# Gated delta rule in a hybrid decoder block: the keys' matrix split from the queries', blocks of 32 instead of 16, and another projection order

## The chip, the cores and the metric

One core of one Trainium2 chip runs the whole kernel. The metric is device microseconds of one execution. The kernel before takes 711.61 us, the median of three runs from 710.02 to 714.58 us. Everything is float32 at the edges; the large products run as three passes over a high and a low part (`mm3`), and what is called f32 below on TensorE without such a split runs as two instructions for each matmul.

## The reference

One layer of a decoder block over 1024 tokens of width 1024. Half of the mixer is stick-breaking attention (8 heads of 64), half a gated delta rule (4 heads of 128, chunks of 64 in the reference):

```python
h = rmsnorm(x, norm1_w);  proj = h @ w_in                     # 1024 x 4104
sb_q, sb_k, sb_v, sb_z, g_q, g_k, g_v, g_z, g_b, g_a = split(proj)
# stick-breaking: A[t,s] = sigmoid(z_ts) * prod_{s<j<t} (1 - sigmoid(z_tj)),  o = A v
# delta rule, after a causal convolution of 4 taps, silu, and l2norm of q and k:
a_mat = where(strict, (k_beta @ k.T) * decay, 0)              # of one chunk
sol   = triangular_solve(a_mat + eye, [v_beta, k_beta*exp(g)], unit lower)
attn_intra = where(incl, (q @ k.T) * decay, 0)
for chunk: v_new = u - w @ S;  o = (q*exp(g)) @ S + attn_intra @ v_new
           S = S*exp(g_last) + (k*exp(g_last-g)).T @ v_new
x = x + concat(rmsnorm(o_sb)*silu(sb_z), rmsnorm(o_gdn)*silu(g_z)) @ w_out;  return rmsnorm(x)
```

## The kernel before

The kernel writes chunks of 128 tokens, so a delta head has 8 chunks, treated as two units of 4 (`g` = 0 and 1; unit `u = 2h+g`). All work is written as generators ("streams"): the scan over chunks (`delta_scan`, priority 0), the inversion (`delta_solve`), the substitution (`delta_blocks`), what precedes them (`delta_pre`), attention, the projections (`fill`, priority 100), and the output product (`product`, 101). A recording layer (`Model`) prices each instruction with `cost`, lets the streams go on when what they wait for has ended by these prices, and so fixes the order of every engine's instructions at build time. On the chip each engine then runs its list in order and waits on semaphores. All recorded instructions carry line L316, so rows are told apart by the names of their tiles.

Projections run in the order of `ORDER`: `v0`, `v1` are halves of attention's values with gates' columns, `k0`..`k3` attention's keys (two heads each), `G0`..`G3` a delta head (three column blocks: k, then q, then v; kinds 1, 0, 2), `z0`..`z7` the output gates. Each column block is 48 TensorE matmuls of 512 columns in two halves. Its weights are split by ScalarE (`weh`) and GpSimd (`wel`). TensorE gets its matmuls from attention and the delta rule as they become ready, and from the projections in between; attention starts when `v1` and the decays are done.

One delta head goes through these steps:

- `gdn_norms`: transposes of k and q (`kq`), squares summed by ScalarE, one reciprocal root for both (`rkq`).
- `gdn_pre`: for each chunk one matmul of k against k and q together (256 columns), from it the negated keys' matrix `nm` (in the buffer `dt`) and the queries' matrix `at`. It starts when the head's k, q and (part of) v are projected.
- `gdn_blocks`: the 32 diagonal blocks of 32x32 of a head (8 chunks, 4 blocks each) go to DRAM (`bd`) and come back with a block's matrix on the partitions that work on it (`br`). `xs` is the inverse being built by forward substitution, two columns a step: a product `tm` over what is there, then a sum of it. The kernel before inverts the two 16x16 halves of each block this way (8 steps, `tm` of 32 to 256 columns, all on VectorE), and joins the halves with two groups of 32 small matmuls: `y0p` (tile rows `pz<-wc,dt`, 16 rows) and `x0p` (`pz<-yt,xc`).
- `gdn_inv`, for each unit: joins blocks of 32 to 64 and to 128 (`xinv`) with small matmuls, starting with `pz<-wc,dt` of 32 rows; `gdn_chain`: the scan over 4 chunks.

`product` multiplies the mixed outputs by `w_out` in 8 token blocks of 128. Its first two blocks take the halves in the order (0, delta half), (1, delta half), (0, attention half), (1, attention half); the sums of block 0 stand in the two PSUM buffers `pp` that the projections use too, those of block 1 in `pz`. The weights of the attention half (`wol`) are split after the last projection, in the memory of the projections' input.

Of the kernel before, what the change touches and what calls it, by code (L numbers as in the profile page):

```python
# [17 lines left out]
P = 128  # L18
T = 1024
D = 1024  # L20
NB = T // P
# [8 lines left out]
ORDER = "v0 k0 v1 G0 k1 G1 k2 G2 G3 k3 z0 z1 z2 z3 z4 z5 z6 z7".split()  # L30
# [393 lines left out]
def block(tc, xT_d, x_d, n1_d, wE_d, wQ_d, wC_d, conv_d, alog_d, dtb_d, mixw_d, wo_d, fnw_d, out_d):  # L424
# [4 lines left out]
    with ExitStack() as top:  # L429
# [23 lines left out]
        n1 = cst.tile([P, NK], F32, name="n1")  # L453
        conv = cst.tile([P, 12, 4], F32, name="conv")
        mixw = cst.tile([P, NK], F32, name="mixw")
        alog = cst.tile([P, GH], F32, name="alog")
        dtb = cst.tile([P, GH], F32, name="dtb")
        x0 = cst.tile([P, 8, 16], F32, name="x0")
        low = cst.tile([P, 1], F32, name="low")
        rstd = cst.tile([P, NB], F32, name="rstd")  # L460
        rs8 = cst.tile([P, NB], F32, name="rs8")
        ns8 = cst.tile([P, NB], F32, name="ns8")
        rbc = cst.tile([P, T], F32, name="rbc")
        make_identity(nc, ident)
        sel = cst.tile([P, P], F32, name="sel")
        V.memset(sel, 0.0)
# [5 lines left out]
        rkq = cst.tile([P, GH, 2, NB], F32, name="rkq")  # L472
# [12 lines left out]
        xd0 = dr.tile([16, 16], F32, name="xd0")  # L485
        xds = [dr.tile([32 * 1024 + 528], F32, name=f"xd{i}") for i in range(2)]
# [53 lines left out]
        ones, triu, zero = [sm[:, i * P:(i + 1) * P] for i in range(3)]  # L540
# [68 lines left out]
        def row_scale(half, dgs):  # L609
            rp = pz()  # L610
            for g, dg in enumerate(dgs):
# [4 lines left out]
        S.dma_start(xd0, ident[0:16, 0:16])  # L616
        S.dma_start(x0.rearrange("p r i -> p (r i)"),
                    xd0.rearrange("(g r) i -> g (r i)", g=2).unsqueeze(0).to_broadcast([64, 2, 128]))
        V.tensor_reduce(low, ident.rearrange("p (q u i) -> p q u i", u=2, i=16)[:, :, 1, :], AX.XY, ALU.add)
        V.memset(zero, 0.0)  # L620
        for t in xds:
            for u in range(2):
                S.dma_start(t[16384 * u:16384 * u + 16384].rearrange("(p f) -> p f", p=P), zero)
# [7 lines left out]
        xs = gd.tile([P, 8, 32], F32, name="xs")  # L631
        edge = gd.tile([P, 3], F32, name="edge")
        for t in (*xinv, w64, xs):
            G.memset(t, 0.0)
# [31 lines left out]
        def decays(me):  # L666
# [41 lines left out]
            for h in range(GH):  # L708
                for g in range(2):
                    hc = slice(4 * g, 4 * g + 4)  # L710
                    dt = gd.tile([P, 4, P], F32, tag=("at", "nkv")[g], bufs=3, turn=True, name="dt")
# [77 lines left out]
        def projections():  # L789
# [30 lines left out]
            while nxt:  # L820
# [7 lines left out]
                for half in range(2):  # L828
# [15 lines left out]
                    if half == 0:  # L844
                        if name[0] == "G":
# [32 lines left out]


        def delta_blocks():  # L880
            for h in range(GH):
                yield lambda: h == 0 or f"i{2 * h - 1}" in flags
# [10 lines left out]
        def delta_scan():  # L893
# [7 lines left out]
            rq = rkq[:, :, 1]  # L901
# [9 lines left out]
        def gdn_norms(h):  # L911

            ss = gd.tile([P, 2, NB], F32, tag="ss", name="ss")
            kns = []
            for g in range(2):
                kq = gst[h]["kq"][g]
                kns.append(gd.tile([P, 4, P], F32, tag="kn", bufs=4, turn=True, name="kn"))
                for which in range(2):
                    tp = pz()
                    for j in range(4):  # L920
                        TE.transpose(tp[:, j * P:(j + 1) * P], kq[:, j, which, :], ident)
                    if which == 0:
                        A.activation(kns[g].rearrange("p c d -> p (c d)"), tp, AF.Copy)

                    for j in range(4):
                        js = tp[:, j * P:(j + 1) * P]
                        A.activation(js, js, AF.Square, accum_out=ss[:, which, 4 * g + j:4 * g + j + 1])
                    yield
            V.tensor_scalar(ss, ss, EPS, None, ALU.add)
            rr = rkq[:, h]  # L930
            _rsqrt(V, gd, rr.rearrange("p a c -> p (a c)"), ss.rearrange("p a c -> p (a c)"), 2 * NB, "rru")
            r2b = gd.tile([P, NB], F32, tag="r2b", bufs=2, turn=True, name="r2b")
            V.tensor_tensor(r2b, rr[:, 0, :], rr[:, 0, :], ALU.mult)
# [3 lines left out]
            nk = gd.tile([P, NB], F32, tag="nk", name="nk")  # L937
            V.tensor_tensor(nk, ss[:, 0, :], rr[:, 0, :], ALU.mult)
# [6 lines left out]

        def gdn_pre(h, g):
            st = gst[h, g]
            kq, vt = gst[h]["kq"][g], gst[h]["vt"]
            kn, nk, mr2b = st["kn"], st["nk"], st["mr2b"]
            cs = slice(4 * g, 4 * g + 4)  # L950
            dt = gd.tile([P, 4, P], F32, tag="dt", bufs=2, name="dt")
            S.dma_start(dt, dt_s[h, g])
            nkv = gd.tile([P, 4, P], F32, tag="nkv", bufs=3, turn=True, name="nkv")
            S.dma_start(nkv, cum_s[1, h, cs].partition_broadcast(P))
            nm = dt
            at = gd.tile([P, 4, P], F32, tag="at", bufs=3, turn=True, name="at")
            for i in range(2):
                gpt = pz()
                for j in range(2):
                    c = 2 * i + j  # L960
                    TE.matmul(gpt[:, j * 256:(j + 1) * 256], kq[:, c, 0, :], kq[:, c, :, :].rearrange("p a t -> p (a t)"),
                              start=True, stop=True)
                gv = gpt.rearrange("p (j a t) -> p j a t", j=2, a=2)
                V.tensor_tensor(at[:, 2 * i:2 * i + 2, :], gv[:, :, 1, :], dt[:, 2 * i:2 * i + 2, :], ALU.mult)
                for j in range(2):
                    c = 2 * i + j
                    r = V.scalar_tensor_tensor(nm[:, c, :], gpt[:, j * 256:j * 256 + P], mr2b[:, c:c + 1], dt[:, c, :], ALU.mult, ALU.mult)
                yield
            st.update(nkv=nkv, nm=nm, at=at)
            flags[f"p{2 * h + g}"] = r  # L970
# [6 lines left out]
            for j in range(4):  # L977
                A.activation(nkv[:, j, :], tp[:, j * P:(j + 1) * P], AF.Copy, scale=nk[:, j:j + 1])
            flags[f"q{2 * h + g}"] = r
            yield  # L980

        def gdn_blocks(h):
            bd = dr.tile([32, 32, 32], F32, tag="bd", bufs=2, name="bd")
            xd = xds[h % 2]
# [5 lines left out]
            br = gd.tile([P, 16, 32], F32, tag="br", name="br")  # L990
            bf = br.rearrange("p k i -> p (k i)")
            for u in range(2):
                S.dma_start(bf[64 * u:64 * u + 64, 0:496],
                            bd.rearrange("n k i -> n (k i)")[:, 528 * u:528 * u + 496].unsqueeze(1).to_broadcast([32, 2, 496]))
            V.memset(bf[:, 0:496:66], 0.0)
            V.memset(bf[:, 33:496:66], 1.0)
            V.tensor_copy(xs[:, :, 0:16], x0)
            tm = gd.tile([P, 256], F32, tag="tm", name="tm")
            fold = tm[:, 0:98].rearrange("p (k m) -> p k m", m=7)
            V.tensor_tensor(fold, br[:, 0:14, 2:16:2], bf[:, 67:496:66].unsqueeze(1).to_broadcast([P, 14, 7]), ALU.mult)  # L1000
            V.tensor_tensor(br[:, 0:14, 3:16:2], br[:, 0:14, 3:16:2], fold, ALU.add)
            V.memset(bf[:, 0:496:66], 1.0)
            for i in range(0, 16, 2):
                n = i + 2
                tm = gd.tile([P, 256], F32, tag="tm", name="tm")
# [4 lines left out]
            for u in range(2):  # L1010
                dst = xd[528 * u:528 * u + 32768].rearrange("(n g f) -> n g f", g=4, f=256)[:, 0:2, 0:240]
                S.dma_start(dst, xs.rearrange("p r i -> p (r i)")[64 * u:64 * u + 64, 0:240])
            xc = gd.tile([P, 8, 32], F32, tag="xc", name="xc")
            yield S.dma_start(xc, xd[0:32768].rearrange("(c b r i) -> (b r) c i", b=4, r=32, i=32))
            wc = gd.tile([P, 8, 32], F32, tag="wc", name="wc")
            yield V.transpose(wc.rearrange("p c i -> p (c i)"), xc.rearrange("p c i -> p (c i)"))

            quads = [slice(32 * q, 32 * q + 32) for q in range(4)]
            y0p = pz()
            yv = y0p[:, 0:256].rearrange("p (c i) -> p c i", c=8)  # L1020
            for q in range(4):
                for c in range(8):
                    TE.matmul(yv[quads[q], c, :], gst[h, c // 4]["nm"][32 * q:32 * q + 16, c % 4, quads[q]], wc[32 * q:32 * q + 16, c, :], start=True, stop=True)
# [456 lines left out]
```

## Time and profile before

| what | value |
|---|---|
| median of 3 runs | 711.61 us (710.02 to 714.58) |
| the profiled execution | 713.0 us, span of its instructions 711.3 us |
| granted TensorE clock, mean | 0.983 |
| busy: TensorE / VectorE / ScalarE / GpSimd | 684.5 / 473.3 / 382.1 / 264.1 us |
| the 256 matmuls that the diff takes out, TensorE busy | 7.6 + 8.6 us (256 instructions each) |

A row of the profile's groups gives engine, operation, tiles (out, then in), shape, count, busy time and the mean duration of one, then the idle time of that engine before the group and what ended it. Busy time of TensorE counts a matmul from its start to the modelled end, so that the time between the starts of two rows is what one costs where they follow each other without a wait.

### The profile page before, as it was taken

Reading aid. Unit: us, or ns where it says so; the run is one execution under the profiler, and the core shown is the slowest. Engines: PE = TensorE matmul, PEld = TensorE weight load, DVE = VectorE, ACT = ScalarE, POOL = GpSimd, SP = SyncE. Lnnn points to the kernel's source line nnn. Section 1 sums busy time; section 2 is a strip of 40 time slices with the busy share of each in tenths; the row PEclk is TensorE's granted clock in tenths of the full one; section 3 lists DMA queues with packets and bytes.
Section 4 is the critical chain, followed back from the end, with each engine's and each line's share of the span. In section 5 each row is a group of like instructions: output and inputs, shape, how many; then the busy total and the mean of one; then the engine's idle time right before and its main releaser. Section 6 shows DMA issues by size and latency. Waiting matters only on the chain.

```text
span 711.3 us, 12623 instructions
## 1 busy us (share of the span) xinstructions
PE 684.5 (96%) x4446; PEld 575.9 (81%) x4446; DVE 473.3 (67%) x1042; ACT 382.1 (54%) x961; POOL 264.1 (37%) x230
## 2 busy tenths in 40 slices
PE   8999999999999899989999999999999999699996
PEld 7889898787888788877888787888978887577885
DVE  5354512968898685997778974549678563576653
ACT  5662154984757857668686654348685442221212
POOL 0002063655435045542326531337423245323421
PEclk9999999999999999999999998999999999899998
DMA  8937279233641153620513211273421388446531
GB/s 301 370 107 280 88 253 308 79 116 106 176 115 36 31 171 89 209 56 9 164 42 105 75 45 41 88 251 103 129 61 42 105 266 298 135 139 209 171 130 59
DMA packets 80078, 98.80 MB, mean 139 GB/s; under 512 B 17584, under 2 KB 50320, under 8 KB 80016
## 3 DMA queue, kind: packets, MB, share of 16 engines
q1 hardware_dynamic: 80016, 98.01, 42.9%
q8 instruction: 35, 0.57, 0.3%
q14 instruction: 27, 0.22, 0.1%
HBM read 69.87 MB, written 28.12 MB: 138 GB/s over the span
## 4 chain that ended last, share of the span: by engine, by line
PE 75%; DVE 7%; ACT 7%; DMA 4%; issue 4%; POOL 2%; SPq 1%; POOLq 0%; ACTq 0%; DVEq 0%
PE pp L316 45%; PE pz L316 22%; PE po L316 5%; PE pc L316 3%; ACT pz L316 2%; DMA rb<-rs_s 1%; DVE cc L316 1%; ACT sg L316 1%; ACT xinv L316 1%; DMA fnw<-fnw 1%; SPq L316 1%; DVE al L316 1%; DMA dt<-cum_s 1%; POOL wel L316 1%; POOL dt L316 1%
## 5 line engine op out<-in xcount | busy, mean ns | idle before, releaser
L316 PE MATMUL pp<-xh,weh 128*128 128x512 f32 x384 | 164.0, 427 | 3.1 <-DVE pre L316 2.2
L316 PE MATMUL pp<-xh,wel 128*128 128x512 f32 x384 | 151.8, 395 | 0.1
L316 PE MATMUL pp<-xl,weh 128*128 128x512 f32 x384 | 151.2, 394 | 0.0
L316 POOL TENSOR_TENSOR sg<-sg,cc 128x128 f32<-128x128 f32 (+3 forms) x64 | 78.0, 1221 | 102.1 <-DVE cc L316 97.5
L316 POOL TENSOR_TENSOR wel<-wer,weh 128x512 fp32r<-128x512 f32 x48 | 63.1, 1317 | 96.6 <-ACT weh L316 92.1
L316 PEld LDWEIGHTS pp<-xh,wel 128*128 128x128 f32 x384 | 72.5, 189 | 17.0 <-POOL wel L316 0.5
L316 PEld LDWEIGHTS pp<-xh,weh 128*128 128x128 f32 x384 | 72.9, 190 | 15.1 <-ACT oe L316 2.3
L316 PEld LDWEIGHTS pp<-xl,weh 128*128 128x128 f32 x384 | 73.1, 190 | 9.8
L316 DVE TENSOR_TENSOR_SCAN cc<-pz,step 128x384 f32<-128x384 f32 (+2 forms) x64 | 53.5, 845 | 12.6 <-ACT pz L316 10.9
L316 ACT ACTIVATE sg<-pz,rs 128x384 f32<-128x384 f32 (+3 forms) x96 | 53.8, 589 | 9.0 <-PE pz L316 8.3
L316 DVE TENSOR_TENSOR al<-pz,ah 128x512 fp32r<-128x512 f32 (+1 forms) x80 | 49.7, 628 | 12.8 <-ACT ah L316 12.4
L316 ACT ACTIVATE ah<-pz 128x512 fp32r<-128x512 f32 (+1 forms) x80 | 43.5, 558 | 27.2 <-PE pz L316 26.6
L316 PE MATMUL pp<-woh,mh 128*128 128x512 f32 (+1 forms) x120 | 47.0, 392 | 6.8 <-DVE zt L316 6.2
L316 ACT ACTIVATE pz<-pz,ns 128x384 f32<-128x384 f32 (+3 forms) x96 | 51.8, 564 | 0.2
L316 PE MATMUL pp<-woh,ml 128*128 128x512 f32 (+1 forms) x120 | 46.3, 386 | 0.7 <-POOL ml L316 0.6
L316 PE MATMUL pp<-chl,xh 128*128 128x264 f32 (+1 forms) x256 | 46.6, 284 | 0.0
L316 PE MATMUL pp<-wol,mh 128*128 128x512 f32 (+1 forms) x120 | 46.2, 385 | 0.0
L316 PE MATMUL pz<-step,sg 128*128 128x128 f32 x288 | 43.9, 277 | 0.1
L316 PE MATMUL po<-ah,v2a 128*128 128x256 f32 (+1 forms) x160 | 42.3, 288 | 0.0
L316 DVE TENSOR_TENSOR_SCAN cc<-pz,cc,step 128x512 f32<-128x512 f32 (+1 forms) x32 | 38.7, 1208 | 3.6 <-ACT pz L316 3.1
L316 POOL TENSOR_TENSOR ml<-mf,mh 128x512 fp32r<-128x512 f32 x16 | 20.5, 1287 | 54.0 <-ACT mh L316 54.0
L316 PEld LDWEIGHTS pp<-chl,xh 128*128 128x128 f32 x256 | 39.7, 188 | 0.3
(245 smaller groups left out, 1550.7 us busy)
## 6 DMA issues: line engine op xcount, KB each, us to landing
wer<-wE SPq DMA_DIRECT2D x48, 256.0 KB
xr<-x SPq DMA_DIRECT2D x16, 512.0 KB
qk_s<-xq SPq DMA_DIRECT2D x8, 512.0 KB
v_s<-v2e SPq DMA_DIRECT2D x16, 256.0 KB
q<-qk_s SPq DMA_DIRECT2D x8, 512.0 KB
kh<-qk_s SPq DMA_DIRECT2D x8, 512.0 KB
kl<-qk_s SPq DMA_DIRECT2D x8, 512.0 KB
v2a<-v_s SPq DMA_DIRECT2D x8, 512.0 KB
```

The source lines that it names most:

```text
L316: ins = f(*args, **kw).ins
```

## The change

The projections' order starts with the delta head 0 (`G0`) ahead of `v1` and `k1`. `delta_pre` now waits only for a head's k (`G{h}1`): `gdn_norms` transposes and squares k alone, and `gdn_pre` multiplies k by k (128 columns a chunk) and makes `nm`. A new stream `delta_late` (priority 0.65) does the queries' squares (`query_norms`, with one reciprocal root for all heads at the end), and the queries' matrix (k against q, 128 columns a chunk), the scaled q and the values' transposes (`gdn_late`). `nm` has four buffers, and `gdn_blocks` no longer waits for the inversion of the head before at its start, only before it reads its result back.

In `gdn_blocks` the substitution goes over whole blocks of 32: 16 steps with `tm` of 32 to 512 columns. The products go from VectorE to GpSimd (`G.tensor_tensor`), the sums stay on VectorE. The two groups of small matmuls that joined halves of 16 are gone, as are the zeroed DRAM buffers. `product` puts the sums of block 0 into the PSUM buffers `po` and `pc`, which attention and the scan use. Small constants now share one tile `sel`.

```diff
-ORDER = "v0 k0 v1 G0 k1 G1 k2 G2 G3 k3 z0 z1 z2 z3 z4 z5 z6 z7".split()
+ORDER = "v0 k0 G0 v1 k1 G1 k2 G2 G3 k3 z0 z1 z2 z3 z4 z5 z6 z7".split()
...
+                        if name[0] == "G" and name[2] == "2":
+                            yield lambda: name[1] == "0" or f"q{2 * int(name[1]) - 1}" in flags
...
-                yield from until(f"G{h}0")
+                yield from until(f"G{h}1")
                 yield lambda: h < 2 or f"c{2 * h - 3}" in flags
                 yield from gdn_norms(h)
                 for g in range(2):
                     u = 2 * h + g
+                    yield lambda: u < 4 or f"i{u - 4}" in flags
+                    yield from gdn_pre(h, g)
+        def delta_late():
+            for h in range(GH):
+                yield from until(f"G{h}0")
+                yield lambda: f"p{2 * h}" in flags
+                yield from query_norms(h)
+                for g in range(2):
+                    u = 2 * h + g
                     yield from until(f"G{h}2" if g else f"G{h}2.0")
-                    yield lambda: (u < 2 or f"i{u - 2}" in flags) and (u < 3 or f"c{u - 3}" in flags)
-                    yield from gdn_pre(h, g)
+                    yield lambda: f"p{u}" in flags and (u < 2 or f"c{u - 2}" in flags)
+                    yield from gdn_late(h, g)
...
+        def gdn_pre(h, g):
+            kq, mr2b = gst[h]["kq"][g], gst[h, g]["mr2b"]
+            nm = gd.tile([P, 4, P], F32, tag="dt", bufs=4, turn=True, name="dt")
+            S.dma_start(nm, dt_s[h, g])
+            gpt = pz()
+            for j in range(4):
+                TE.matmul(gpt[:, j * P:(j + 1) * P], kq[:, j, 0, :], kq[:, j, 0, :], start=True, stop=True)
+            for j in range(4):
+                r = V.scalar_tensor_tensor(nm[:, j, :], gpt[:, j * P:(j + 1) * P], mr2b[:, j:j + 1], nm[:, j, :], ALU.mult, ALU.mult)
...
+        def gdn_late(h, g):
+            nkv = gd.tile([P, 4, P], F32, tag="nkv", bufs=2, turn=True, name="nkv")
+            S.dma_start(nkv, cum_s[1, h, 4 * g:4 * g + 4].partition_broadcast(P))
+            at = gd.tile([P, 4, P], F32, tag="at", bufs=2, turn=True, name="at")
+            S.dma_start(at, dt_s[h, g])
+            for j in range(4):
+                TE.matmul(gpt[:, j * P:(j + 1) * P], kq[:, j, 0, :], kq[:, j, 1, :], start=True, stop=True)
+            V.tensor_tensor(af, gpt, af, ALU.mult)
...
-            for i in range(0, 16, 2):
+            for i in range(0, 32, 2):
                 n = i + 2
-                tm = gd.tile([P, 256], F32, tag="tm", name="tm")
+                tm = gd.tile([P, 512], F32, tag="tm", name="tm")
                 tv = tm[:, 0:16 * n].rearrange("p (r u k) -> p r u k", r=8, u=2)
-                V.tensor_tensor(tv, xs[:, :, 0:n].unsqueeze(2).to_broadcast([P, 8, 2, n]),
+                G.tensor_tensor(tv, xs[:, :, 0:n].unsqueeze(2).to_broadcast([P, 8, 2, n]),
                                 br[:, 0:n, i:i + 2].rearrange("p k u -> p u k").unsqueeze(1).to_broadcast([P, 8, 2, n]), ALU.mult)
                 V.tensor_reduce(xs[:, :, i:i + 2], tv, AX.X, ALU.add)
...
+            yield lambda: h == 0 or f"i{2 * h - 1}" in flags
...
-                    TE.matmul(yv[quads[q], c, :], gst[h, c // 4]["nm"][32 * q:32 * q + 16, c % 4, quads[q]], wc[32 * q:32 * q + 16, c, :], start=True, stop=True)
-            yield V.tensor_scalar(yt, yv, low[:, 0:1], None, ALU.mult)
-                    TE.matmul(xv[quads[q], c, :], xc[quads[q], c, :], yt[quads[q], c, :], start=True, stop=True)
-            V.tensor_tensor(wc, xv, wc, ALU.add)
...
-                        tag = ("pp", "pz")[b == 1]
-                        ys[b, n] = (pp, pz)[b == 1]()[:, 0:w]
+                        tag, bufs = ("pp", 2) if b > 1 else ("pz", 4) if b else (("po", "pc")[n], 1)
+                        ys[b, n] = pst(tag, bufs)[:, 0:w]
```

TensorE where head 0 is inverted, in the kernel before. `pp` rows are projections, `po<-a..` and `pz<-step,sg` attention; `pz<-wc,dt 32x32 x32` and `pz<-yt,xc` are the two groups of 32 matmuls that join halves of 16 (of the first, 16 of 32 rows are used), `pz<-wc,dt 32x32 x8` begins `gdn_inv`.

```order
L316 MATMUL pp<-xh,wel 128x512
L316 MATMUL pz<-wc,dt 32x32 x32
L316 MATMUL pz<-oe,sel 128x256
L316 MATMUL pz<-step,sg 128x128 x3
L316 MATMUL pp<-xh,weh 128x512
L316 MATMUL pp<-xl,weh 128x512
L316 MATMUL pp<-xh,wel 128x512
L316 MATMUL po<-ah,v2a 128x256
L316 MATMUL po<-al,v2a 128x256
L316 MATMUL po<-ah,v2a 128x256
L316 MATMUL po<-al,v2a 128x256
L316 MATMUL pz<-yt,xc 32x32 x32
```

The same place on TensorE in the changed kernel, up to the product of 64 (`pz<-w..,dt`).

```order
L316 MATMUL pz<-step,sg 128x128 x4
L316 MATMUL pz<-wc,dt 32x32 x8
L316 MATMUL pp<-xh,weh 128x512
L316 MATMUL pp<-xl,weh 128x512
L316 MATMUL pp<-xh,wel 128x512
L316 MATMUL pz<-xc,y_2194 32x32 x8
L316 MATMUL pz<-y_2194,xc 32x32 x4
```

The groups of 32 are gone; `gdn_inv` follows attention's and the projections' matmuls directly.

GpSimd in the late steps of head 0's substitution, in the changed kernel. `sg` rows are attention's weights, which TensorE transposes next, `wel` rows the low part of a projection's weights, `kt` is an attention key.

```order
L316 TENSOR_TENSOR tm<-xs,br 128x352
L316 TENSOR_TENSOR sg<-sg,cc 128x128
L316 TENSOR_TENSOR sg<-sg,cc 128x256
L316 TENSOR_TENSOR tm<-xs,br 128x384
L316 TENSOR_TENSOR sg<-sg,cc 128x384
L316 TENSOR_TENSOR sg<-sg,cc 128x512
L316 TENSOR_TENSOR tm<-xs,br 128x416
L316 TENSOR_TENSOR kt<-kt,sqh 128x512
L316 TENSOR_TENSOR sg<-sg,cc 128x640
L316 TENSOR_TENSOR tm<-xs,br 128x448
L316 TENSOR_TENSOR wel<-wer,weh 128x512
```

In the kernel before none of the `tm` rows stand on this engine. Now each waits for the sum that VectorE made of the one before, and what attention and the projections need stands behind it.

TensorE at the end of the projections in the changed kernel: the last projection matmul and the first of the output product.

```order
L316 MATMUL pp<-xh,weh 128x512
L316 MATMUL pp<-xl,weh 128x512
L316 MATMUL pp<-xh,wel 128x512
L316 MATMUL po<-woh_6642,mh 128x512
L316 MATMUL po<-wol_6643,mh 128x512
L316 MATMUL po<-woh_6642,ml 128x512
```

In the kernel before, the last three write `pp`: block 0 takes both buffers, one for each 512 output columns, and the second is still held by the last projection until `zt` has been read out of it.

More of the change, by code (lines that the diff above doesn't have):

```diff
@@ L452, in block @@
         ident = step[:, 384:512]
[L453 to L462, printed above, removed]
+        sel = cst.tile([P, P], F32, name="sel")
+        conv = sel[:, 2:50].rearrange("p (a b) -> p a b", b=4)
+        n1, mixw, rstd, rs8, ns8, al2 = [sel[:, 50 + 8 * i:58 + 8 * i] for i in range(6)]
+        alog, dtb = al2[:, 0:GH], al2[:, GH:]
         rbc = cst.tile([P, T], F32, name="rbc")
         make_identity(nc, ident)
-        sel = cst.tile([P, P], F32, name="sel")
-        V.memset(sel, 0.0)
+        V.memset(sel[:, 98:P], 0.0)
         V.tensor_reduce(sel[:, 0:2], ident.rearrange("p (h d) -> p h d", h=2), AX.X, ALU.add)
@@ L471, in block @@
         ssg = cst.tile([P, GH, NB], F32, name="ssg")
-        rkq = cst.tile([P, GH, 2, NB], F32, name="rkq")
+        rk = cst.tile([P, GH, NB], F32, name="rk")
+        rq = cst.tile([P, GH, NB], F32, name="rq")
+        ssq = cst.tile([P, GH, NB], F32, name="ssq")
         gsc = {n: cst.tile([P, GH, NB], F32, name=n) for n in ("beta", "cum", "eg", "neg", "egl", "kd")}
@@ L539, in block @@
         sm = at_.tile([P, 768], F32, tag="sg5", name="sm")
-        ones, triu, zero = [sm[:, i * P:(i + 1) * P] for i in range(3)]
+        ones, triu = [sm[:, i * P:(i + 1) * P] for i in range(2)]
         ga = sm[:, 384:448].rearrange("p (b e) -> p b e", e=8)
@@ L613, in row_scale @@
             V.tensor_copy(rbc[:, 512 * half:512 * half + 512], rp)
[L616 to L623, printed above, removed]
+        S.dma_start(xd0, ident[0:32, 0:32])
         s0_ctx.close()
@@ L630, in block @@
         w64 = gd.tile([64, 4, 64], F32, name="w64")
-        xs = gd.tile([P, 8, 32], F32, name="xs")
         edge = gd.tile([P, 3], F32, name="edge")
-        for t in (*xinv, w64, xs):
+        for t in (*xinv, w64):
             G.memset(t, 0.0)
@@ L900, in delta_scan @@
                     flags[f"c{u}"] = True
-            rq = rkq[:, :, 1]
+            yield lambda: "rq" in flags
             t0 = gd.tile([P, GH, NB], F32, tag="yt", name="t0")
@@ L944, in gdn_norms @@
             yield r
-        def gdn_pre(h, g):
-            st = gst[h, g]
[L948 to L970, printed above, removed]
@@ L978, in gdn_pre @@
                 A.activation(nkv[:, j, :], tp[:, j * P:(j + 1) * P], AF.Copy, scale=nk[:, j:j + 1])
+            st.update(nkv=nkv, at=at)
             flags[f"q{2 * h + g}"] = r
@@ L1439, in block @@
                    [Stream(delta_scan(), 0, DELTA), Stream(delta_solve(), 0.5, DELTA + 0.5), Stream(delta_blocks(), 0.6, DELTA + 0.6),
-                    pre, Stream(attention(), 9.995, WINDOW), Stream(out_weights(), -3, OUT_WEIGHTS), fill,
+                    pre, Stream(delta_late(), 0.65, DELTA + 0.65), Stream(attention(), 9.995, WINDOW), Stream(out_weights(), -3, OUT_WEIGHTS), fill,
                     Stream(mixed_delta(), -2, OUTPUT), Stream(factors(), -1, 4), Stream(prepare(), 50, DELTA), Stream(product(), 101, DELTA)])
```

103 lines of the change are left out of this document (52 added, 51 removed).

## The prediction

> **What bounds the kernel now.** The first two parts of the profile's page say which engine to look at, and whether it is the same one all along.
>
> ```profile
> PE 684.5 (96%) x4446; PEld 575.9 (81%) x4446; DVE 473.3 (67%) x1042; ACT 382.1 (54%) x961; POOL 264.1 (37%) x230
> PE   8999999999999899989999999999999999699996
> ```
>
> TensorE is busy in every slice but the first, one near 600 us and the last. A busy TensorE need not be a late one, so I take the long middle part, where attention and the delta rule run, and the end of the projections from the view by windows (span, then busy time of TensorE, weight loads, VectorE, ScalarE, GpSimd, then the clock).
>
> ```profile
> 125.00:562.00 437.00, 427.09 (x3130) 358.10 (x3130) 334.81 (x734) 288.94 (x802) 184.81 (x148) 0.98 0.32 97
> 602.00:645.00 43.00, 35.55 (x147) 27.96 (x147) 27.42 (x51) 10.11 (x14) 12.08 (x11) 0.92 0.49 150
> ```
>
> In the middle TensorE is without work for 9.9 us in 437; VectorE has 23% left, ScalarE 34%, GpSimd 58%. So time that leaves TensorE's list there leaves the run, as long as nobody else becomes late. From 602 to 645 it lacks 7.4 us. The view of waits says what it waited for.
>
> ```profile
> PE pp L316 <- DVE zt L316: 6.4, 2, 6.2
> PE pz L316 <- ACT xinv L316: 1.7, 2, 1.0
> PE pz L316 <- DVE rkq L316: 1.2, 1, 1.2
> PE pz L316 <- DVE w L316: 1.1, 2, 1.0
> ```
>
> One wait of 6.2 us stands out; the delta rule's waits are about 1 us each. The engine is a list in a fixed order with almost no holes, and the forecast is a sum over that list.
>
> **The small matmuls go.** From the timeline of TensorE, head 0:
>
> ```profile
> 219.08 0.39 PE L316 MATMUL pp<-xl,weh 128*128 128x512 f32 x1
> 219.31 0.40 PE L316 MATMUL pp<-xh,wel 128*128 128x512 f32 x1
> 219.64 1.91 PE L316 MATMUL pz<-wc,dt 16*32 16x32 f32 x64
> 221.48 0.70 PE L316 MATMUL pz<-oe,sel 128*128 128x256 f32 x2
> ...
> 223.60 1.91 PE L316 MATMUL pz<-yt,xc 32*32 32x32 f32 x64
> 225.44 0.66 PE L316 MATMUL pz<-step,sg 128*128 128x128 f32 x4
> ```
>
> From start to next start the groups cost 221.48 - 219.64 = 1.84 and 225.44 - 223.60 = 1.84 us. The projection matmul ahead of the first takes 0.33 us where its neighbour takes 0.23, so entering such a group costs about 0.1. Four heads, two groups: 4 x (3.68 + 0.2) = 15.5 us, all of it on TensorE's path. The groups' busy times in the view by lines (7.6 and 8.6 us) give 16.2, nearly the same.
>
> **Keys and queries apart.** 32 matmuls of 256 columns become 64 of 128, with as many columns but twice the weight loads.
>
> ```profile
> 169.34 1.03 PE L316 MATMUL pz<-kq 128*128 128x256 f32 x4
> 170.01 0.58 PE L316 MATMUL pp<-xh,weh 128*128 128x512 f32 x1
> ...
> 548.59 0.38 PE L316 MATMUL pz<-v,kn 128*128 128x128 f32 x2
> 548.81 0.39 PE L316 MATMUL pz<-state,kq 128*128 128x128 f32 x2
> ```
>
> A group of 4 instructions of 256 columns took 0.67 us; 128-column ones take 0.22 a pair (548.59 to 548.81). 16 groups at 0.67 are 10.7 us, 64 pairs at 0.22 are 14.1: +3.4. Bounds: nothing, if they go at the 0.168 of two such halves, up to the +9 that 64 isolated pairs of 0.39 (25) would give over the 16.5 of busy time. The new matmuls stand four in a row, so I take the 0.22, less the wider groups that took longer than this one: +2.4.
>
> **The wait near 604 us.** Rows of TensorE, then of VectorE, then windows with the granted clock (third number from the end):
>
> ```profile
> 604.35 0.39 PE L316 MATMUL pp<-woh,ml 128*128 128x512 f32 x1
> 610.89 0.80 PE L316 MATMUL pp<-woh,mh 128*128 128x512 f32 x1 [6.16 <-DVE zt L316]
> ...
> 603.22 5.82 DVE L316 SCALAR_TENSOR_TENSOR wol<-wor,mixw,woh 128x1024 fp32r<-128x1024 f32 x4 [5.83 <-ACT woh L316]
> 608.96 1.28 DVE L316 TENSOR_TENSOR mf<-oa,rb 128x512 f32<-128x512 f32 x2
> 610.16 0.68 DVE L316 TENSOR_TENSOR zt<-pp,rbc 128x512 f32<-128x512 f32 x1
> ...
> 611.00:613.00 2.00, 2.00 (x5) 1.63 (x6) 2.00 (x3) 0.56 (x1) 2.00 (x3) 0.50 0.57 161
> 613.00:616.00 3.00, 3.00 (x10) 2.36 (x10) 1.20 (x1) 0.00 (x0) 1.12 (x1) 0.63 0.59 112
> 616.00:620.00 4.00, 4.00 (x19) 3.24 (x18) 0.00 (x0) 0.00 (x0) 0.00 (x0) 1.00 0.04 12
> ```
>
> Block 0's second sum needs the `pp` buffer that the last projection still holds; its reading (`zt`) stands on VectorE behind four weight splits and two `mf`. With `po` and `pc` that need is gone: -6.2 us. After the wait the clock was granted at 0.50 for 2 us and 0.63 for 3 us, which costs 1.0 + 1.1 = 2.1 more: -8.3 together. The Trainium skill ("TensorE: Matmul & The Clock Gate", Part 1, What's actually happening) says the array falls to half rate after an idle window of about 3.4 us; the 0.50 row agrees. What is late next: 48 matmuls of 0.23 (the spacing of the 219 us rows) fill 11 us; the last projection stands 12 matmuls before the end of the 604.35 row, so at 601.8, and the splits end 7.2 us after it (603.22 + 5.82), the parts of block 1 later, at about 11. I put +0.5 for that. If cover fails here, the price is a second wait of some 3 us.
>
> **The substitution.** Its steps go from 8 to 16 and its products to GpSimd. Rows of head 1 by time, then groups:
>
> ```profile
> 275.07 3.17 SPq L316 DMA_DIRECT2D bd<-dt x4
> ...
> 287.10 0.70 DVE L316 TENSOR_TENSOR tm<-br 128x98 f32<-128x98 f32 x1
> 305.11 0.41 DVE L316 TENSOR_REDUCE xs<-tm 128x16 f32<-128x256 f32 x1
> 314.52 0.41 DVE L316 STREAM_TRANSPOSE wc<-xc 128x256 f32<-128x256 f32 x1
> ...
> L316 DVE TENSOR_TENSOR tm<-xs,br 128x256 f32<-128x256 f32 x4 | 2.7, 674 | 0.0
> L316 DVE TENSOR_REDUCE xs<-tm 128x16 f32<-128x256 f32 x4 | 1.6, 401 | 0.0
> L316 DVE TENSOR_TENSOR mf<-oa,rb 128x512 f32<-128x512 f32 x8 | 5.4, 683 | 1.7 <-POOL rb L316 1.7
> L316 POOL TENSOR_TENSOR kq<-kq,nkv 128x512 f32<-128x512 f32 x8 | 10.3, 1282 | 4.3 <-PE pz L316 4.3
> ```
>
> A head's products have 16 x (2+4+...+32) = 4352 columns, against 1152. At GpSimd's 1282/512 = 2.5 ns that is 10.9 us a head, plus some 2 for the two folding steps: about 52 us more on an engine that has 252 us free in the middle. VectorE loses its products and gains eight longer sums, a balance near zero. The chain of one head now takes 18.4 us for 8 steps, most of it waiting between other instructions. Sixteen steps that cross engines twice each I put at 40 to 45. Transfers lie ahead and behind: 12 us from the last blocks' write to the first fold, 9 from the last sum to `wc`. Together 61 to 66 us. None of it has a place on TensorE's list; its cover is the work that stands there between a head's keys' matrix and its inversion. In the changed order of head 1 these are 185 matmuls of 512 columns (0.23 us each, 42.6), 58 of 256 (0.12, 7.0), 66 transposes (0.09, 5.9), 41 f32 pairs (0.22 to 0.32, 9.4) and 28 narrower split ones (3.1): 68 us. The 0.12 and the 0.09 are from these rows:
>
> ```profile
> 222.01 0.49 PE L316 MATMUL pz<-step,sg 128*128 128x128 f32 x3
> 222.26 0.48 PE L316 MATMUL pp<-xh,weh 128*128 128x512 f32 x1
> ...
> 223.04 0.28 PE L316 MATMUL po<-ah,v2a 128*128 128x256 f32 x1
> 223.16 0.28 PE L316 MATMUL po<-al,v2a 128*128 128x256 f32 x1
> ```
>
> The cover is thin. Bounds: no new wait, or every microsecond that the products take longer, four times. For the contiguous rate I take +1.5 in all, since the waits before at these places are about 1 us each, and one of them (`rkq`) goes with the small matmuls.
>
> Nothing else costs TensorE time: moving `G0` ahead of `v1` and `k1` moves 33 us of projections (144 x 0.23); attention starts that much later and must still end before the projections do. Its cover is the projections left over when it ends, one run of 32 us in the kernel before:
>
> ```profile
> 561.87 31.98 PE pp L316 x141
> ```
>
> In the changed order 66 projection matmuls (15 us) stand behind attention's last, so the cover shrinks but lasts. The order has four more function-table loads on ScalarE, beside `G0`:
>
> ```profile
> L316 ACT ACT_TABLE_LOAD x4 | 5.1, 1283 | 0.8 <-PEq L1455 0.8
> ```
>
> They cost TensorE nothing while ScalarE has room; without it 4 x 1.3 us, which is within the bounds. The decay matrices are read twice (8 more loads of 256 KB), while the zeroed buffers and their transfers go; the windows above have the DMA engines at 0.32 in the middle, so I put nothing. SP's queue runs in order: blocks (`bd`) that wait for a late `nm` hold back the weights' loads behind them, which is part of the slower rival below.
>
> **Sum.** The profiled execution took 713.0 us, 1.4 above the median. -15.5 + 2.4 - 8.3 + 0.5 + 1.5 = -19.4; 713.0 - 19.4 - 1.4 = **692** against the median.
>
> **Rivals.**
>
> *Strided products* (mid-way). VectorE took 674 ns for 256 columns of `tm`, of which one operand is read at a stride of 32 elements, and 683 for 512 contiguous ones: twice as much a column. If GpSimd pays half of that, 4352 x 1.25 ns = 5.4 us a head. The 2 to 7 us between chain and cover hide a part, and 2 a head show: 692 + 8 = 700. For it: the operand is the same. Against: GpSimd's 2.5 ns may be bound elsewhere. The Trainium skill ("GPSIMD Engine Reference", Performance pitfalls for Q7 kernels) has such a rule: a stride above 8 bytes costs about half more. No run so far shows it; by it this rival holds.
>
> *Substitution late everywhere* (slower). If GpSimd pays the full factor of two, 10.9 us a head come on top. TensorE waits at each of the four inversions, and `sg` and `wel`, which stand behind `tm` rows on GpSimd, are late with it: 692 + 4 x 7 = 720, and up to 736 with no slack. It decides from about 2.5 + 2 = 4.5 ns a column. Against it: VectorE's products also ran late before, with no more than 1.2 us of waits.
>
> *TensorE not the limit.* If ScalarE or VectorE set attention's pace in the middle, only the 8 us at the end are gained: 705. Against it the 23% and 34% of room.
>
> **Chances.** Forecast (686 to 698) 0.62; strided products 0.18; late everywhere 0.11; not the limit 0.09. Most of the second case is still under 704.5. Range 683 to 711: the low end is all waits in the middle halved, the high end takes in the second and fourth case. A change within 1% (704.5 to 718.7) is about what a measurement of this kernel cannot tell from none. Faster 0.76, same 0.14, slower 0.10.
>
> **What would show it.** No `pz<-wc,dt 16*32` and `pz<-yt,xc` rows; no wait for `zt` and no clock of 0.50 after the projections; `tm` on GpSimd of 512 columns near 1.3 us (forecast), 1.9 (second case) or 2.6 (third); waits of TensorE for `xc`/`wc` or `sg` no longer than now. Waits of 5 us and more at the inversions, or a hole before the output product, would make the forecast wrong.

## The result and the profile after

The changed kernel took **687.16 us** (median of 4 runs, 684.06 to 689.90) beside 710.82 us for the kernel before in the same comparison; the ratio is 0.966, with a 95% interval of 0.960 to 0.972. The profiled execution took 687.9 us with a span of 686.2; before it was 713.0 and 711.3.

The page of the changed kernel, TensorE's first lines (busy time and share of the span, then the busy tenths in 40 slices):

```profile
PE 664.5 (97%) x3998; PEld 561.0 (82%) x3998; DVE 477.0 (70%) x1019; ACT 384.3 (56%) x965; POOL 331.3 (48%) x301
PE   8999999999999999999999999999999999989995
```

TensorE's busy time fell by 20.0 us and its idle time by 5.1 (26.8 to 21.7). GpSimd took on 67 us, VectorE 4. The slice near 600 us is full now. The same two windows as before, and one more; then three of the kernel before:

```profile
125.00:562.00 437.00, 427.59 (x2830) 363.05 (x2829) 332.22 (x678) 292.64 (x795) 254.04 (x224) 0.99 0.40 126
602.00:645.00 43.00, 40.92 (x186) 32.84 (x185) 30.16 (x79) 9.34 (x16) 16.80 (x16) 1.00 0.70 209
205.00:212.00 7.00, 7.00 (x50) 5.84 (x48) 5.53 (x14) 4.54 (x13) 1.97 (x2) 0.52 0.00 1
...
243.00:246.50 3.50, 3.50 (x12) 2.94 (x12) 1.96 (x11) 2.69 (x8) 0.00 (x0) 0.52 0.15 37
328.50:332.00 3.50, 3.50 (x28) 2.81 (x25) 2.81 (x4) 2.68 (x6) 1.06 (x2) 0.51 0.00 0
427.50:434.30 6.80, 6.80 (x84) 5.70 (x80) 3.31 (x12) 2.74 (x8) 1.30 (x1) 0.50 0.06 12
```

In the middle TensorE lacks 9.4 us of 437, as good as before (9.9): what was gained there is list and clock, and no waiting went. The other rows are about the clock. In the trace's record it has two values, 1.00 and 0.50, and 0.50 lasts 3.41 us or a whole multiple of that. One such piece costs half of the time in it that TensorE is busy, so at most 1.7 us. Up to the last matmul the kernel before has 6 of them: one, one and two in the last three rows, and two from 608.4 us on, behind the wait for `zt`, of which TensorE was still idle for 2.5 us. They cost 4 x 1.7 + 2.2 = 9.0 us. The changed kernel has 2, both in the third row, 3.4 us; so 5.6 of the 25.1 us are the clock. The Trainium skill ("TensorE: Matmul & The Clock Gate", Part 1, What's actually happening) gives the same two states and a free-running window of 3413 ns; the record agrees.

What TensorE waits for now (total, times, longest):

```profile
PE pz L316 <- DVE cc L316: 3.6, 6, 1.3
PE pp L316 <- DVE pre L316: 1.6, 3, 0.8
PE po L316 <- POOL step masks.py:199: 1.4, 1, 1.4
PE pp L316 <- ACT mh L316: 1.4, 1, 1.4
```

`zt`, `rkq` and `xinv` are gone from the top. New is `cc`, attention's running sums on VectorE. From the groups, the keys' and queries' products, and the longest product of the substitution:

```profile
L316 PE MATMUL pz<-kq 128*128 128x128 f32 x128 | 17.0, 277 | 0.0
L316 POOL TENSOR_TENSOR tm<-xs,br 128x512 f32<-128x512 f32 x4 | 6.3, 1577 | 0.8 <-DVE xs L316 0.8
```

The time is thus 25.1 = 5.6 (clock) + 5.1 (idle) + 14.5 (list), rounded. This is one execution of each kernel; two executions of one list, shown below, differ by 1.9 us before any of the changed work begins, so a term is known to about 2 us. The experiments ask which edit brought which.

### The profile page after: what moved, and what is told of

It reads as the page before. It is cut to its first block, busy times and chain, and to the rows that moved or that the text cites. A ratio compares the mean times of both kernels' runs of the same rounds, so it can differ in the third digit from the quotient of the medians.

```text
span 686.2 us, 11753 instructions
## 1 busy us (share of the span) xinstructions
PE 664.5 (97%) x3998; PEld 561.0 (82%) x3998; DVE 477.0 (70%) x1019; ACT 384.3 (56%) x965; POOL 331.3 (48%) x301
## 4 chain that ended last, share of the span: by engine, by line
PE 62%; POOL 11%; DVE 10%; ACT 7%; issue 5%; DMA 4%; SPq 1%; POOLq 0%; DVEq 0%; ACTq 0%
PE pp L316 37%; PE pz L316 17%; POOL tm L316 6%; PE po L316 5%; PE pc L316 3%; DVE cc L316 3%; ACT pz L316 2%; DMA wer<-wE 1%; DVE pp L316 1%; POOL wel L316 1%; POOL sg L316 1%; DMA rb<-rs_s 1%; SPq L316 1%; DVE al L316 1%; DVE xs L316 1%
## 5 line engine op out<-in xcount | busy, mean ns | idle before, releaser
L316 PE MATMUL pp<-xh,weh 128*128 128x512 f32 x384 | 160.5, 418 | 0.7 <-DVE pre L316 0.7
L316 POOL TENSOR_TENSOR tm<-xs,br 128x32 f32<-128x32 f32 (+7 forms) x64 | 59.4, 928 | 8.9 <-DVE xs L316 8.3
L316 ACT ACTIVATE sg<-pz,sel 128x384 f32<-128x384 f32 (+3 forms) x96 | 53.6, 587 | 13.1 <-PE pz L316 12.1
L316 ACT ACTIVATE pz<-pz,sel 128x384 f32<-128x384 f32 (+3 forms) x96 | 52.1, 564 | 0.0
L316 DVE TENSOR_REDUCE xs<-tm 128x16 f32<-128x32 f32 (+7 forms) x64 | 27.7, 433 | 26.1 <-POOL tm L316 25.8
L316 PE MATMUL po<-ah,v2a 128*128 128x256 f32 (+1 forms) x160 | 43.7, 296 | 0.0
L316 DVE SCALAR_TENSOR_TENSOR pp<-pre,sel,pp 128x512 f32<-128x512 f32 x48 | 35.9, 749 | 7.6 <-ACT pp L316 7.3
L316 PE MATMUL pp<-woh,mh 128*128 128x512 f32 (+1 forms) x104 | 39.6, 381 | 1.4 <-ACT mh L316 1.4
L316 PE MATMUL po<-al,v2a 128*128 128x256 f32 (+1 forms) x160 | 39.8, 284 | 1.2 <-DVE al L316 1.1
```

What stands on the lines that cost most here:

```text
L316: ins = f(*args, **kw).ins
```

## The experiments

**The wait at the end.** Block 0 put back on `pp`, and the other way round:

```diff
-  tag, bufs = ("pp", 2) if b > 1 else ("pz", 4) if b else (("po", "pc")[n], 1)
+  tag = ("pp", "pz")[b == 1]
```

> The changed kernel with block 0 of the output product back on the pp buffers. List theory (the time is TensorE's list plus the few waits on it, each edit counted by itself): the wait for zt of about 6 us and the half clock behind it come back, 687 + 8 = 695 us. Overlap theory (the gain is from the streams' new order, which ends everything else earlier, VectorE's readings too): zt is no longer late, 687 to 689 us.

> The kernel before with only block 0's sums on po and pc. List theory: 711 - 8 = 703 us, no wait for zt, no clock of 0.50 near 611 us. Overlap theory: the wait moves to the next late reading, 708 to 711 us.

In the changed kernel it made no difference: 685.42 us (684.23 to 688.04; ratio to before 0.957 to 0.964). In the kernel before it was worth what the list theory says: 704.42 against 712.64 us (ratio 0.987, 0.983 to 0.991), and TensorE's longest waits there are then (`pre` is the convolution's input, read out of a delta head's projection)

```profile
PE pp L316 <- DVE pre L316: 2.3, 2, 1.9
PE pz L316 <- ACT xinv L316: 1.7, 2, 1.0
```

So the edit can take the wait away, and in the changed kernel it was not needed. VectorE's rows of the first experiment by time say why:

```profile
580.70 0.69 DVE L316 TENSOR_TENSOR zt<-pp,rbc 128x512 f32<-128x512 f32 x1 [0.37 <-PE pp L316]
582.07 6.98 DVE L316 SCALAR_TENSOR_TENSOR wol<-wor,sel,woh 128x1024 fp32r<-128x1024 f32 x4 [0.68 <-ACT woh L316]
588.97 0.68 DVE L316 TENSOR_TENSOR mf<-oa,rb 128x512 f32<-128x512 f32 x1
```

`zt` now stands ahead of the four weight splits; before it stood behind them (603.22, then 610.16). `pp` is free 0.7 us after the last projection.

**The small matmuls taken from the kernel before.** In `gdn_blocks` (`yt` and its two readings go with them):

```diff
-  TE.matmul(yv[quads[q], c, :], nm[...], wc[32 * q:32 * q + 16, c, :])   # 32 calls
-  TE.matmul(xv[quads[q], c, :], xc[quads[q], c, :], yt[quads[q], c, :])  # 32 calls
```

> The kernel before without the 128 small matmuls a head and without their two readings on VectorE (the part of the inverse blocks that joins the two halves is left out). List theory: 711 - 15.5 = 695 us, or 1 to 2 us less, since one wait of 1.2 us for rkq goes too. Overlap theory: not under 705 us, since the substitution and the keys' matrix come as late as before.

694.56 against 712.64 us: -18.1 (ratio 0.973, 0.969 to 0.977). The four pieces at 0.50 in the middle are gone, and four stand behind a wait at the end, with TensorE idle in part of them. Between the two profiled executions, 18.8 us apart, the clock is 4.9 by the count above, the list 15.2, and TensorE is idle 1.3 longer. The one long wait, in TensorE's rows (`mx` is the delta half of the mixed outputs, being scaled):

```profile
584.27 0.45 PE L316 MATMUL pz<-step,mx 128*128 128x128 f32 x1 [6.20 <-DVE mx L316]
```

Three of the four splits stand ahead of `mx` this time (579.29 to 582.96 on VectorE). Overlap theory falls, and the end's wait turns out to be a matter of what happens to stand behind those splits on VectorE.

**The small matmuls put back into the changed kernel,** back to back:

```diff
   r = V.transpose(wc..., xc...)
+  yield r
+  # 32 calls pz<-dt,wc of 16 rows, yield, 32 calls pz<-xc,wc of 32 rows
```

> The changed kernel with the 128 small matmuls a head put back on TensorE at their old shapes, in two groups behind the inverse blocks; their sums are read by nobody. List theory: 8 groups of 1.84 + 0.1 us, 687 + 15.5 = 702 to 703 us. Overlap theory (small matmuls lie in time that TensorE has to spare beside the substitution's chain): 687 to 691 us.

Four runs of 712.88, 725.14, 729.12 and 732.10 us, with mean granted clocks of 0.971, 0.950, 0.949 and 0.942. Only the first, at the highest clock, is compared: +26 us, well over the list's 15.5. Neither theory had that. Time follows the clock from run to run of one program; so a third theory: short matmuls close together lower the clock. Two kernels test it, the small groups apart, and full-size ones of equal length in their place:

```diff
+  yield V.tensor_copy(yt, yv)      # between the two groups, as before
```

```diff
+  for u in range(2):
+      for k in range(8): TE.matmul(pz, xh[:, k, 0:128], xh[:, k, 0:512])
```

> The changed kernel with the 128 small matmuls a head put back, the second group reading what VectorE copied from the first, as before, so that other matmuls stand between the groups; the last sums are read by a copy that nobody uses. Clock theory (small matmuls close together lower the granted clock, and back to back they cost 35 us of half clock where the list alone says 15.5): apart they cost 15.5 to 20, 702 to 707 us, mean clock over 0.98. Rival (the added matmuls cost that much by themselves or by the waits around them): 715 us or more, clock below 0.97.

> The changed kernel with 16 split matmuls of 512 columns a head in the place of the 128 small ones (16 x 0.23 = 3.7 us a head, as long as those), sums read by nobody. List theory: 687 + 14.7 = 702 us. Clock theory for the small ones: the same 702 us with no new stretch at half clock (mean clock 0.99), so the difference to the small ones put back to back is the clock alone. Rival (TensorE has spare time there): 687 to 691 us.

Apart: 706.93 us median (ratio 0.989, 0.985 to 0.994). Of ten runs three took 700.2 to 702.0 us at clocks of 0.992 to 0.994, six 705.6 to 707.5 at 0.985 to 0.987, and one 716.82 at 0.967. At the high clock the small matmuls cost 13 to 15 us, near the list's 15.5; the rest goes with the clock. Wide: 704.26 us (703.31 to 707.60), clocks 0.991 to 0.994, one piece at 0.50. The row of one head's:

```profile
196.92 4.14 PE L316 MATMUL pz<-xh 128*128 128x512 f32 x16
```

16 a head, 0.25 us each, give 16 of the 17 us, so TensorE has no time to spare there, and as much of wide work doesn't lower the clock.

**Rows or shortness.** The two groups with all 128 rows and columns of `nm` as weights, 32 columns moving as before:

```diff
+  TE.matmul(y0p[:, 32 * c:32 * c + 32], nm[:, c % 4, :], wc[:, c, :])    # 2 x 32 calls
```

> The changed kernel with two groups of 32 products a head back to back, at the place of the small ones and with as many columns each (32), but with all 128 rows and columns of the keys' matrix as weights; sums read by nobody. Row theory (it is the few rows and columns of the array in use that lower the granted clock): the list grows by about 64 x 0.045 us a group, 687 + 23 = 710 us, and the clock stays at 0.99. Rival (it is the short instructions, however many rows they use): as many stretches of 0.50 as with the small ones put back to back (21 of 3.4 us), 735 us or more, clock below 0.96.

808.57 us (803.89 to 814.01; ratio 1.134), clock 0.90, 45 pieces. The row theory falls. TensorE's row, then windows (the third number from the end is the clock):

```profile
196.95 8.35 PE L316 MATMUL pz<-wc,dt 128*128 128x32 f32 x54
...
196.00:198.00 2.00, 2.00 (x21) 2.00 (x19) 0.00 (x0) 2.00 (x11) 1.10 (x1) 1.00 0.00 0
198.00:200.00 2.00, 2.00 (x21) 2.00 (x20) 0.77 (x4) 2.00 (x11) 0.00 (x0) 1.00 0.04 8
200.00:202.00 2.00, 2.00 (x14) 2.00 (x13) 2.00 (x7) 0.23 (x1) 0.00 (x0) 0.62 0.00 0
202.00:204.00 2.00, 2.00 (x11) 2.00 (x11) 1.44 (x6) 1.22 (x4) 0.56 (x1) 0.50 0.00 0
```

TensorE is busy all through, and 4 us after the first such matmul the clock is halved. An instruction of this kind takes 0.095 us at clock 1.00 (21 in 2 us) and 0.18 at 0.50 (11 in 2 us), not the 0.045 expected. So 512 of them are 49 us of list, and most of the remaining 73 us is the clock (45 pieces against 2). What these and the small ones share is 32 moving columns for each load of weights.

The traces say more about what the throttle may count. Take every 3.41 us window of the clock's record at 1.00 in the 14 profiled executions, and add up the moving columns in it, each weighted by the share of 128 rows that its matmul uses. Of 37 windows ahead of a fall to 0.50, 36 have at most 2350 such columns, and of the 2660 others 11; the median of those is 6800. Busy time doesn't tell them apart: in 13 of the 37 TensorE was busy for over 3.3 us. So an idle window and one full of short matmuls look alike by this sum. That is a count over traces; no run varied it alone.

**The order alone, and the delta rule alone.**

```diff
-ORDER = "v0 k0 v1 G0 k1 ...    (kernel before)
+ORDER = "v0 k0 G0 v1 k1 ...
```

The second kernel is the changed one with the old `ORDER` and block 0 on `pp`.

> The kernel before with the new projection order alone. Order theory (block 0's wait for zt went because the new order ends attention and the projections at other times, so that zt and the weight splits are no longer last): 711 - 8 = 703 us and no wait for zt. Rival (the wait went through the other edits of the delta rule): 709 to 713 us, the wait of about 6 us stays.

> The changed kernel with the old projection order and block 0 back on pp: only the delta rule's edits are left. Order theory: the wait for zt is back, 687 + 8 = 695 us. Rival (the delta rule's edits alone took it away): 685 to 689 us. If neither order nor buffers matter the gain is all the delta rule's.

The order alone makes the kernel before *slower*, 741.01 against 711.32 us (ratio 1.039, 1.030 to 1.047). It has 23 pieces at 0.50, 17 more than before, which by the count above cost up to 26 of the 29.7 us. Fifteen of them follow a window full of small matmuls, the other eight one in which TensorE was idle for more than half. The wait for `zt` is gone, as the order theory has it, but one of 6.2 us for `mx` stands at its place. TensorE's rows at the last head's small groups, then its windows:

```profile
541.24 1.91 PE L316 MATMUL pz<-wc,dt 16*32 16x32 f32 x64
...
543.97 1.91 PE L316 MATMUL pz<-yt,xc 32*32 32x32 f32 x64
545.81 1.22 PE L316 MATMUL pz<-oe,sel 128*128 128x256 f32 x2
...
541.00:546.00 5.00, 5.00 (x134) 4.27 (x133) 1.93 (x11) 0.42 (x1) 0.00 (x0) 0.98 0.48 161
546.00:552.00 6.00, 6.00 (x49) 4.19 (x50) 2.01 (x6) 1.85 (x6) 0.00 (x0) 0.50 0.04 4
552.00:573.00 21.00, 21.00 (x111) 16.00 (x111) 6.39 (x22) 6.74 (x20) 3.81 (x3) 0.50 0.05 17
```

Here only 0.9 us of projections stand between the two groups (543.08 to 543.97), where head 0 of the kernel before has 2.1. TensorE never stops, the clock goes to 0.50 just as the second group ends, and it stays there for 8 pieces, in which the inversion's own small matmuls follow.

The delta rule's edits alone give 698.62 us, -12.7 (ratio 0.980, 0.973 to 0.986), with no wait for `zt`: they suffice to move it, without order or buffers. Against the changed kernel with block 0 on `pp` (685.42), from which it differs by the order alone, it lacks 13.2 us. The profiled execution, the slowest of its four at 701.38 us, has 6 pieces at 0.50 against 1 (7.7 of 16.2 us between the two profiled), and waits for a projection's split weights on GpSimd, which aren't on the other's list:

```profile
PE pp L316 <- POOL wel L316: 3.8, 3, 2.6
```

So the same order is +30 us in the kernel before and -13 in the one with the delta rule's edits. That the small matmuls make the difference fits the fifteen pieces, but the two kernels differ in the other edits too, and no run took the small matmuls alone out under the new order.

**The products.** On VectorE in GpSimd's place, and then on GpSimd with a contiguous operand:

```diff
-  G.tensor_tensor(tv, xs[:, :, 0:n]..., br[:, 0:n, i:i + 2]...)
+  V.tensor_tensor(tv, xs[:, :, 0:n]..., br[:, 0:n, i:i + 2]...)
```

```diff
-  br[:, 0:n, i:i + 2].rearrange("p k u -> p u k").unsqueeze(1)
+  br[:, i:i + 2, 0:n].unsqueeze(1)
```

> The changed kernel with the 64 products on VectorE in GpSimd's place (the fold stays on GpSimd). At the 2.4 ns a column that VectorE took for them before, 42 us more on VectorE, 59 us less on GpSimd. Cover theory (the substitution lies beside TensorE's list on either engine): 685 to 690 us. Rival (VectorE, 70 per cent busy, is then late for attention): waits for cc and al grow by 1 to 2 us a head, half clock follows, 694 us or more.

> The changed kernel with the products' second operand read along its rows, contiguous, in the place of the stride of 32 elements (the values are then those of the wrong rows, so the inverse blocks are not the reference's). Stride theory: the product of 512 columns falls from 1577 to about 1280 ns, the rate of the contiguous one of the same engine; 11 us less on GpSimd. If the cover is as wide as the trace says, the time stays at 685 to 689 us; if it is thin, 4 us less. Rival (the rate is bound by two operands, not by the stride): 1577 ns stays.

On VectorE: 712.93 us (709.19 to 717.79), as slow as the kernel before. The engine has room on average, yet the middle window shows TensorE 25 us short of 437, and the waits name VectorE:

```profile
125.00:562.00 437.00, 411.85 (x2718) 345.62 (x2717) 365.68 (x728) 285.10 (x772) 192.71 (x149) 0.98 0.38 118
...
PE pp L316 <- DVE pre L316: 6.7, 6, 1.8
PE pz L316 <- DVE cc L316: 5.5, 10, 1.4
PE pz L316 <- DVE rk L316: 2.5, 2, 1.3
```

Contiguous: 677.84 us (677.36 to 679.64; ratio 0.951, 0.949 to 0.954). All five engines run the same list as in the changed kernel, but for two neighbours on VectorE in exchanged order, so the two can be laid side by side. Its longest product, then `cc` among its waits:

```profile
L316 POOL TENSOR_TENSOR tm<-xs,br 128x512 f32<-128x512 f32 x4 | 5.1, 1286 | 0.8 <-DVE xs L316 0.8
...
PE pz L316 <- DVE cc L316: 1.1, 4, 0.5
```

The stride cost 23% (1577 against 1286). All 64 products took 59.4 us and now take 49.6; the median is 9.3 lower, and at equal clock (0.998, one run each: 684.06 and 678.07) 6.0. Side by side, TensorE's starts in the two profiled executions drift apart by 1.9 us before the first product, by 2.3 where the changed kernel has its half clock, and by 2.0, 1.8, 2.2 and 0.3 from a head's first product to its `wc`. These 6.3 us are the substitution's. Cover is thin, then, though TensorE never waits for `xc` or `wc`. How the pace gets to TensorE, in the changed kernel's rows of three engines:

```profile
168.27 1.16 POOL L316 TENSOR_TENSOR tm<-xs,br 128x352 f32<-128x352 f32 x1
...
167.49 0.68 DVE L316 TENSOR_TENSOR kt<-pp,rbc 128x512 f32<-128x512 f32 x1
169.46 0.52 DVE L316 TENSOR_REDUCE xs<-tm 128x16 f32<-128x352 f32 x1 [1.28 <-POOL tm L316]
169.90 2.06 DVE L316 TENSOR_TENSOR_SCAN cc<-pz,step 128x384 f32<-128x384 f32 x2
...
170.90 0.55 PE L316 MATMUL pz<-step,sg 128*128 128x128 f32 x3 [1.27 <-DVE cc L316]
```

VectorE stands 1.28 us before a sum whose product isn't there. Attention's scan `cc`, ready to run, is queued behind that sum, `sg` is made from it, and TensorE waits 1.27 us. With the contiguous operand the same place costs TensorE 0.25:

```profile
166.36 0.52 DVE L316 TENSOR_REDUCE xs<-tm 128x16 f32<-128x352 f32 x1 [1.09 <-POOL tm L316]
...
167.80 0.55 PE L316 MATMUL pz<-step,sg 128*128 128x128 f32 x3 [0.25 <-DVE cc L316]
```

**Fewer changes between kinds of rows,** in the hope of a better kernel:

```diff
-  if k < NK - 1:
+  if k % 2 and k < NK - 1:
       yield
```

> The changed kernel with the projections given out six matmuls at a time instead of three, so that TensorE changes 315 times between split and plain rows instead of 343. List theory: 28 changes of about 0.1 us, 687 - 3 = 684 us. Rival (what stands behind the longer pieces comes 0.7 us later each time, and the waits eat it): 687 to 692 us.

690.69 us (689.58 to 691.15; ratio 0.966 to 0.971): the rival. One piece at 0.50, but the waits grew (`al` is the low part of attention's weights):

```profile
PE pp L316 <- DVE pre L316: 5.2, 6, 2.2
PE pz L316 <- DVE cc L316: 2.2, 5, 1.1
PE pz L316 <- DVE al L316: 2.1, 4, 1.1
```

No version that does the whole computation beat the changed kernel clearly. What the runs point to, `br` laid out so that the products read it contiguously with the right values, was not tried.

## Why the prediction came out, point by point

692 was forecast and 687.16 measured. Against the profiled 713.0 the sum was -19.4, and -25.1 came.

- **List** (-15.5 for the small matmuls, +2.4 for the split products: -13.1). Measured -14.5 in the balance, and -15.2 for the small ones in the kernel before. The split products are +1.0: from the start of each group to the start of what follows, they took 14.1 us against 13.1 for the undivided ones. The forecast took pairs that stand alone at 0.22; in groups of eight instructions a pair mostly went at 0.20 to 0.24, but most undivided groups took 0.86 or more, not the 0.67 of the one that was read.
- **Clock** (-2.1, behind the one wait). Measured -5.6: the 2.1 came as forecast, and 3.4 more in the middle. This is the term that was mis-sized: I priced half clock only behind an idle TensorE. The experiments show that 32-column matmuls packed closely halve it with TensorE busy, so the small matmuls cost more than their places on the list: without them the kernel before has none of its four pieces in the middle. Only two of those four (427.5 us) follow the groups that went; ahead of the other two stand the inversion's own small matmuls with a short wait, as ahead of the two that the changed kernel still has. The clock accounts for 3.5 of the 5.7 us missed.
- **Waits** (-6.2 + 0.5 + 1.5 = -4.2). Idle time fell by 5.1. The size was right, its working half so: I gave the 6.2 to `po` and `pc`, and they would have done it, but in the changed kernel `zt` stands ahead of the splits anyway, and the delta rule's edits suffice for that. The +0.5 at block 0 came as `mh`, 1.4 against 0.7.
- **Substitution.** The "contiguous rate" was wrong and the rival *strided products* half right: 1.58 us for 512 columns, between 1.3 and 1.9. It cost 6 to 9 us, about what that rival says, at a smaller penalty. The cover that I counted, 68 us between keys' matrix and inversion, held: for head 1 the chain took 65.8 us (225.6 to 291.4) and the inversion began 68.6 us after the keys' matrix. The chain's total was right by parts that were not: sixteen steps took 31 us, not 40 to 45, and the transfers and folds around them the rest. The cost came by another door, VectorE's queue, which I had named for SP and GpSimd and not for this engine. That the total still fell below 692 is because the clock's gain and TensorE's shorter other waits outweighed it.
- **Order** ("moves 33 us of projections", costed at nothing). Measured +30 and -13, by the kernel it is put into. In the changed kernel it was a gain. With the delta rule's edits alone the wait for `zt` goes as well, so the sum's terms (-15.5 + 2.4 - 8.3 + 1.5) would make -19.9 there, and -12.7 came. The total is close to the forecast because the order, a term put at nothing, made up for that: this is luck.
- **The other rivals.** *TensorE not the limit* falls: 14.7 us of added wide matmuls cost 17. *Substitution late everywhere* didn't come; with the products on VectorE something like it did, +26 us, on `pre` and `cc` rather than at the inversions.
- **Signs named beforehand.** The small rows and the `zt` wait are gone, and no 0.50 stands behind the projections. One was too narrow: it watched `xc`, `wc` and `sg`, and the new waits are `cc`.

## What to carry to other kernels

Where one engine's list sets the time, price an edit by its places on that list and then ask what it does to the clock: many short matmuls in a few microseconds cost more than their own time, and putting wide ones between them is worth a try. For a chain that crosses engines, look at what stands behind each waiting instruction in that engine's queue; the chain's own consumer may be well covered while a stranger in the queue is late. An edit that removes a wait can be right by itself and worth nothing beside another; undo it in the new kernel as well as doing it in the old one.

## What was unexpected of the hardware

- The granted clock fell to 0.50 with TensorE busy without a gap (5.00 of 5.00 us ahead of 8 pieces), after 4.6 us that held 128 matmuls of 32 columns and 0.9 us of others; after 16 of 512 columns in 4.1 us it stayed at 1.00. The Trainium skill ("TensorE: Matmul & The Clock Gate", Part 1, What's actually happening) ties half rate to an idle window; here a window full of short matmuls had the same effect, and the weighted columns counted above are low in both (at most 2350 in 36 of 37).
- One program's runs differ by the clock: 700.2 to 716.8 us at mean clocks of 0.994 to 0.967.
- GpSimd paid 23% for one of two operands at a stride of 32 elements (1577 against 1286 ns). The Trainium skill ("GPSIMD Engine Reference", Performance pitfalls for Q7 kernels) has half as much again for reads at a stride of more than 8 bytes; with one operand of two strided the measured price is half of that.
- A plain 128-row matmul instruction with 32 moving columns took 0.095 us at clock 1.00 (21 in 2 us), where a 16-row one takes 0.03 (1.84 us for 64).
